# A list scheduler's table of durations: half-width PSUM instructions, tiny scalar ones and the transfer rate

## The chip, the core and the metric

The kernel runs on one core of a Trainium2 chip. The metric is the device time of one execution in microseconds; the time of a kernel is the median of its runs. TensorE (PE) multiplies matrices, and PEld is its weight load, which overlaps it. VectorE (DVE) and ScalarE (ACT) work element by element, GpSimd (POOL) does a few tiny powers, and SyncE (SP) issues every transfer from HBM.

## What is computed

A sequence of 256 tokens of width 1024 goes through two blocks of two layers each, all in fp32.

```python
def first_block(x, ...):             # DEPTH = 2
    for l in range(DEPTH):
        h = hybrid_layer(h, ...)     # norm, w_in, three attentions A, B, C, silu gates, w_out, residual
    return rms_norm(h, final_g)

def second_block(x, ...):
    for l in range(DEPTH):
        h = rms_norm_2(x, mix_pre_norm[l])
        m = hybrid_mixer(h, ...)     # gated delta rule, pooling, retention, three gated branches, w_out
        x = x + rms_norm_2(m, mix_post_norm[l])
        h = rms_norm_2(x, ffn_pre_norm[l])
        x = x + rms_norm_2(swiglu(h, ...), ffn_post_norm[l])
```

## The kernel before

The tokens are two tiles of 128. A weight matrix comes in pieces of two 128-row blocks by up to 512 columns (512 KB), by `piece`: a transfer into a `raw` tile (4 slots), a cast on ACT into `whi` and the remainder on DVE into `wlo` (7 slots each). Every dense product is three matmuls into an `acc` tile of PSUM (3 slots): high by high, high by low and low by high, so that reduced-precision passes add up to nearly fp32. Attention, transposes and the other small products use `sd` tiles of PSUM (5 slots). The stages follow each other: attention layer 1 (to about 115 us), attention layer 2 (to about 250), mixer, feed-forward, mixer, feed-forward.

The program doesn't run in the order in which it is written. `Prog.record` notes every instruction with what it reads and writes, and gives it a duration by `Prog.cost`. `Prog.schedule` then plays the whole program through: each engine takes, of the instructions whose inputs are ready in this play, the one that was recorded first. An instruction is put in its engine's list at the moment the play reaches it; `emit` writes the lists out, and on the chip each engine runs its list strictly in that order. So the durations of `cost`, and in `schedule` the rate of transfers, decide which instruction stands ahead of which, and nothing else. A duration that is too short lets work come early in a list; if the chip is slower there, the engine waits in front of it with later work behind it.

In `cost`, `n` is the number of elements of a partition, `ps` tells that an operand lies in PSUM, and `shift` is an addition for operands that begin on different partitions. A tile of fewer than 128 partitions is called half-width here; such instructions stand in the attention (`kT`, `qT`, `lo` in `attn` and `ab_T`), in `c_in` (96 and 64 partitions) and in the delta rule. Tiny scalar instructions are those on tiles of one to eight columns (`ty`, `r`, `m` in the rows: the normalisations, the exponents' bounds in `attn`, the gate chain of the mixer). In all lists of rows, `b`, `s`, `tg`, `ty`, `m` and so on are the classes of tiles in `Net`. Every engine instruction is issued in `emit`, so one line number, L389, stands for all of them.

Three places of the program come up again. In `attn` each head is: a matmul of scores into `sd`; `TENSOR_REDUCE ty<-sd` on DVE (the maximum); for the masked heads a tiny `TENSOR_SCALAR ty<-ty,m`; two exponentials on ACT into `tg`; transposes `sd<-c,tg` on PE; a cast and a remainder `tg<-sd,tg`; and matmuls `sd<-tg,b`. After the heads, `gate_T` multiplies by the gates: transposes `sd<-c,s`. In `mixer`, the chain from `bas` to `gg` is a score of tiny DVE instructions in a row, and PE's `sd<-m,kk` reads its end. The tile `pv` has one slot: the parameters of the next layer come into it by a transfer that starts when the last reader of the old ones, `b<-b,pv`, is done, and a DVE instruction `pv<-pv` scales them.

## Time and profile before

| | us |
|---|---|
| median of three runs | 1184.35 |
| the runs | 1182.6 to 1185.31 |
| the profiled execution | 1182.21 |
| its span, from the first instruction to the last | 1180.4 |

What lies around the span is 1.8 us. The profile's "busy" of PE takes matmuls with modelled ends that overlap the next one, so a nearly full PE can still lose time between starts. A matmul's real pace is read from the starts of two neighbours: 512 columns take 0.23 us, 384 take 0.17, 256 take 0.12, and a transpose of 128 takes 0.11. The number in brackets behind a row is the idle time ahead of it and what ended it.

### The profile page before, as it was taken

To read this page: it belongs to the slowest core of one execution; us is meant where nothing else is said; L and a number is where in the kernel's file an instruction comes from. 1 tells how busy PE (TensorE), PEld (TensorE's weight loads), DVE (VectorE), ACT (ScalarE), POOL (GpSimd) and SP (SyncE) were. 2 spreads that over 40 slices of the span, in tenths; PEclk is the share of its full clock that TensorE was granted. 3 is DMA by queue.
4 is the path that set the end of the run, shared out by engine and by line. 5 is a ranking of instruction groups with operands and counts; after the bars stand their busy time and mean duration, and the time that the engine had idled before them with its cause. 6 is when DMAs were issued, how large, how long until landed. Compare 5 with 4: busy or idle time off the path is not lost.

```text
span 1180.4 us, 17325 instructions
## 1 busy us (share of the span) xinstructions
PE 1162.6 (98%) x6308; PEld 985.4 (83%) x6308; DVE 888.1 (75%) x1610; ACT 644.7 (55%) x1194; POOL 51.0 (4%) x73
## 2 busy tenths in 40 slices
PE   8999999999999999999999999999999999999997
PEld 6888898878898888888888888898888888888886
DVE  6999899987789787876665638679888777655642
ACT  6777668764465554565454436455554446544531
POOL 1100010000001000000000001000000101000000
PEclk9999999999999999999999999999999999999999
DMA  7335435645373664446644854544654354654651
GB/s 248 123 113 175 148 113 165 195 132 185 108 233 113 208 192 146 152 141 199 204 163 138 274 194 143 162 144 166 226 183 160 108 178 144 201 190 144 226 184 36
DMA packets 64662, 196.54 MB, mean 167 GB/s; under 512 B 11200, under 2 KB 12608, under 8 KB 64576
## 3 DMA queue, kind: packets, MB, share of 16 engines
q1 hardware_dynamic: 64576, 195.44, 51.1%
q8 instruction: 49, 0.80, 0.3%
q14 instruction: 37, 0.30, 0.1%
HBM read 194.10 MB, written 1.05 MB: 165 GB/s over the span
## 4 chain that ended last, share of the span: by engine, by line
PE 82%; DVE 12%; DMA 2%; ACT 2%; issue 2%; POOL 0%; POOLq 0%; DVEq 0%; ACTq 0%
PE acc L389 68%; PE sd L389 15%; DVE wlo L389 4%; DVE b L389 3%; DVE s L389 2%; DVE ty L389 2%; DVE tg L389 1%; DMA raw<-in_wt 1%; ACT whi L389 1%; DMA pv<-in_pv 1%; ACT b L389 0%; DVE m L389 0%; ACT xh L389 0%; ACT s L389 0%; POOL ty L389 0%
## 5 line engine op out<-in xcount | busy, mean ns | idle before, releaser
L389 DVE TENSOR_TENSOR wlo<-raw,whi 128x1024 fp32r<-128x1024 f32 (+4 forms) x380 | 428.0, 1137 | 123.9 <-ACT whi L389 120.9
L389 ACT CAST whi<-raw 128x1024 fp32r<-128x1024 f32 (+4 forms) x380 | 370.6, 984 | 219.2 <-PE acc L389 156.9
L389 PE MATMUL acc<-whi,xh 128*128 128x512 f32 (+4 forms) x1184 | 444.4, 377 | 3.4 <-ACT whi L389 2.6
L389 PE MATMUL acc<-wlo,xh 128*128 128x512 f32 (+4 forms) x1184 | 442.4, 374 | 1.1 <-DVE wlo L389 1.1
L389 PE MATMUL acc<-whi,xl 128*128 128x512 f32 (+4 forms) x1184 | 442.5, 374 | 0.0
L389 PEld LDWEIGHTS acc<-whi,xh 128*128 128x128 f32 x1184 | 223.0, 189 | 40.7 <-ACT whi L389 3.6
L389 PEld LDWEIGHTS acc<-wlo,xh 128*128 128x128 f32 x1184 | 223.3, 189 | 37.9 <-DVE wlo L389 1.9
L389 PEld LDWEIGHTS acc<-whi,xl 128*128 128x128 f32 x1184 | 223.2, 188 | 37.0 <-DVE xl L389 0.7
L389 PE MATMUL acc<-whi,b 128*128 128x512 f32 x328 | 107.0, 396 | 0.0
L389 PEld LDWEIGHTS acc<-whi,b 128*128 128x128 f32 x328 | 61.1, 188 | 14.3 <-ACT b L389 0.4
L389 POOL TENSOR_TENSOR ty<-ty,m 128x4 f32<-128x4 f32 (+3 forms) x34 | 34.9, 1028 | 856.3 <-DVE ty L389 856.3
L389 PE MATMUL sd<-b,b 128*128 128x128 f32 (+3 forms) x464 | 70.1, 289 | 0.1
L389 PE MATMUL acc<-wlo,b 128*128 128x512 f32 x164 | 65.0, 396 | 0.0
L389 PEld LDWEIGHTS sd<-b,b 128*128 128x128 f32 (+2 forms) x464 | 60.4, 190 | 5.4 <-DVE b L389 2.1
L389 ACT ACTIVATE b<-sd 128x512 fp32r<-128x512 f32 (+3 forms) x44 | 23.7, 538 | 63.0 <-PE sd L389 61.8
L389 ACT ACTIVATE s<-acc,r 128x512 f32<-128x512 f32 (+3 forms) x52 | 31.1, 598 | 42.6 <-PE acc L389 40.9
L389 PE MATMUL acc<-xh,whi 128*128 128x256 f32 x192 | 54.0, 281 | 0.0
L389 PE MATMUL acc<-xl,whi 128*128 128x256 f32 x192 | 53.9, 281 | 0.0
L389 PE MATMUL acc<-xh,wlo 128*128 128x256 f32 x192 | 53.8, 280 | 0.0
L389 PE MATMUL sd<-c,s 128*128 128x128 f32 (+2 forms) x260 | 39.9, 273 | 2.8 <-DVE b L389 1.6
L389 DVE SCALAR_TENSOR_TENSOR b<-sd,b 128x512 fp32r<-128x512 f32 (+3 forms) x44 | 26.9, 616 | 17.7 <-ACT b L389 16.7
L389 PEld LDWEIGHTS sd<-c,s 128*128 128x128 f32 (+2 forms) x260 | 30.9, 138 | 10.4 <-DVE s L389 2.6
(178 smaller groups left out, 1278.4 us busy)
## 6 DMA issues: line engine op xcount, KB each, us to landing
raw<-in_wt SPq DMA_DIRECT2D x308, 512.0 KB
raw<-in_wt SPq DMA_DIRECT2D x40, 256.0 KB
raw<-in_wt SPq DMA_DIRECT2D x16, 384.0 KB
raw<-in_wt SPq DMA_DIRECT2D x8, 352.0 KB
b<-in_gains SPq DMA_DIRECT2D x5, 512.0 KB
raw<-in_wt SPq DMA_DIRECT2D x8, 264.0 KB
b<-in_kd SPq DMA_DIRECT2D x2, 512.0 KB
kk<-in_k SPq DMA_DIRECT2D x1, 832.0 KB
```

Of the source, the lines that this page charges most:

```text
L389: o.inst = getattr(eng[o.eng], o.name)(*[real(a) for a in o.args], **{k: real(v) for k, v in o.kw.items()})
```

## The change

Three numbers of the table change. An instruction with a PSUM operand whose result has fewer than 128 partitions gets 110 ns on top, in place of 85 ns or nothing. A `tensor_scalar` on DVE with at most eight columns has a fixed part of 119 ns in place of 69. A transfer moves 280 bytes per ns in place of 350, so that a piece of 512 KB takes 1.87 us of the play's transfer line in place of 1.50. No instruction is added or removed, and no tile changes.

```diff
         shift = 85 if ps and len({a.box[0][0] for a in o.ins + o.outs if a.shape[0] > 1}) > 1 else 0
+        if ps and o.outs[0].shape[0] < P:
+            shift = 110
...
-            return (0.52 if fast else 1.04) * n + 69 + (0 if o.name == "tensor_tensor" else ptr) + shift
+            return (0.52 if fast else 1.04) * n + (119 if n <= 8 and o.name == "tensor_scalar" else 69) + (0 if o.name == "tensor_tensor" else ptr) + shift
...
-                dma = max(dma, hw + 840) + a.free() * a.shape[0] * 4 / 350.0
+                dma = max(dma, hw + 840) + a.free() * a.shape[0] * 4 / 280.0
```

The lists that come of it differ most in the two attention layers (from the first microseconds to about 290 us) and in the mixers; in the feed-forward layers they are the same but for a few pairs. Four places are shown; numbers in tile names differ between the two kernels for the same tile, and the line L389 is L391 afterwards.

Place one, DVE, the end of the last attention of layer 2. `ty_677` before and `ty_672` after hold the maxima of the heads, and `wlo` are remainders of weight pieces. Before:

```order
L389 TENSOR_SCALAR ty_677_2881<-ty_677_2881,m_394_1670 128x2 x2
L389 SCALAR_TENSOR_TENSOR b_700_2971<-s_720_3054,acc_680_2894 128x384
L389 TENSOR_TENSOR s_724_3071<-b_660_2793,m_656_2773 128x384
L389 TENSOR_TENSOR wlo_726_3076<-raw_689_2928,whi_711_3019 128x1024
L389 TENSOR_TENSOR wlo_730_3090<-raw_697_2956,whi_717_3036 128x1024
L389 TENSOR_TENSOR wlo_734_3106<-raw_709_3008,whi_723_3067 128x1024
L389 TENSOR_TENSOR tg_739_3124<-sd_728_3084,tg_733_3101 128x512
L389 TENSOR_TENSOR tg_742_3131<-sd_732_3098,tg_738_3121 128x512
L389 TENSOR_REDUCE ty_677_2881<-sd_736_3110 128x2
L389 TENSOR_TENSOR wlo_745_3145<-raw_713_3024,whi_735_3108 128x1024
L389 TENSOR_TENSOR b_712_3021<-sd_714_3026,s_743_3137 64x256 x2
L389 TENSOR_SCALAR ty_677_2881<-ty_677_2881,m_394_1670 128x2
```

After:

```order
L391 TENSOR_TENSOR wlo_712_3025<-raw_687_2911,whi_706_2996 128x1024
L391 TENSOR_REDUCE ty_672_2859<-sd_709_3009 128x2
L391 TENSOR_TENSOR s_717_3047<-b_658_2805,m_644_2728 128x384
L391 TENSOR_TENSOR tg_719_3054<-sd_713_3029,tg_716_3044 128x512
L391 TENSOR_SCALAR ty_672_2859<-ty_672_2859,m_396_1685 128x2
L391 TENSOR_TENSOR wlo_721_3063<-raw_691_2935,whi_714_3033 128x1024
L391 TENSOR_TENSOR xl_725_3081<-s_670_2853,xh_720_3061 128x2x128
L391 TENSOR_TENSOR xl_725_3081<-s_671_2856,xh_720_3061 128x2x128
L391 TENSOR_TENSOR b_705_2994<-sd_704_2990,s_723_3072 64x256 x2
L391 TENSOR_REDUCE ty_672_2859<-sd_722_3068 128x2
L391 SCALAR_TENSOR_TENSOR b_710_3016<-s_730_3097,acc_663_2829 128x384
L391 TENSOR_SCALAR ty_672_2859<-ty_672_2859,m_396_1685 128x2
```

Both lists end with the tiny instruction on the last head's maxima. Ahead of it, from the first head of this attention on, the list before has seven remainders of 1024 columns, and the one after has three; four have moved behind it.

The same place on PE: `sd_744`, `sd_749` before (`sd_732`, `sd_740` after) are the gates' transposes, `sd_754` (`sd_739`) the last head's. Before:

```order
L389 MATMUL acc_722_3059<-wlo_703_2985,xh_718_3048 128x512
L389 MATMUL acc_722_3059<-whi_686_2918,xl_721_3056 128x512
L389 MATMUL sd_741_3129<-tg_738_3121,b_520_2186 128x256
L389 MATMUL sd_714_3026<-tg_739_3124,b_520_2186 128x256
L389 MATMUL sd_714_3026<-tg_733_3101,b_520_2186 128x256
L389 MATMUL sd_714_3026<-tg_739_3124,b_520_2186 128x256
L389 MATMUL sd_741_3129<-tg_742_3131,b_520_2186 128x256
L389 MATMUL sd_741_3129<-tg_738_3121,b_520_2186 128x256
L389 MATMUL sd_741_3129<-tg_742_3131,b_520_2186 128x256
L389 MATMUL sd_744_3143<-c_6_73,s_688_2926 128x128 x3
L389 MATMUL sd_749_3158<-c_6_73,s_724_3071 128x128 x3
L389 MATMUL sd_754_3171<-c_6_73,tg_750_3161 128x128 x4
```

After:

```order
L391 MATMUL sd_739_3131<-c_6_73,tg_736_3122 128x128 x2
L391 MATMUL sd_740_3134<-c_6_73,s_717_3047 128x128 x2
L391 MATMUL sd_738_3127<-tg_737_3125,b_522_2193 128x256
L391 MATMUL sd_738_3127<-tg_733_3114,b_522_2193 128x256
L391 MATMUL sd_738_3127<-tg_737_3125,b_522_2193 128x256
L391 MATMUL sd_739_3131<-c_6_73,tg_736_3122 128x128 x2
L391 MATMUL sd_740_3134<-c_6_73,s_717_3047 128x128
L391 MATMUL acc_735_3120<-whi_699_2962,xh_720_3061 128x512
L391 MATMUL acc_735_3120<-wlo_701_2980,xh_720_3061 128x512
L391 MATMUL acc_735_3120<-whi_699_2962,xl_725_3081 128x512
L391 MATMUL acc_728_3087<-wlo_712_3025,xh_720_3061 128x512
L391 MATMUL acc_728_3087<-whi_706_2996,xl_725_3081 128x512
```

Before, the transposes of both gates and of the last head, ten in all, stand in one run with the `acc` products ahead of them. After, the transposes come in pieces with other heads' products between them, and the five `acc` products that close the piece stood, for the same pieces of weights, ahead of this place before.

Place two, DVE, the first heads of the same attention. `ty_677` and `ty_672` are the maxima again; the remainders of 768 columns are the four pieces of one chunk of weights. Before (the chunk's first remainder, `wlo_646`, stands 16 rows ahead of the first row shown):

```order
L389 TENSOR_TENSOR wlo_666_2836<-raw_604_2570,whi_620_2628 128x768
L389 SCALAR_TENSOR_TENSOR b_661_2797<-sd_649_2743,b_661_2797 64x3x128
L389 SCALAR_TENSOR_TENSOR b_660_2793<-s_669_2843,acc_657_2775 128x384
L389 TENSOR_TENSOR s_674_2867<-b_563_2411,sd_667_2838 128x256
L389 TENSOR_TENSOR b_655_2767<-sd_649_2743,b_655_2767 64x128 x2
L389 TENSOR_TENSOR s_675_2876<-b_563_2411,sd_670_2845 128x256
L389 TENSOR_REDUCE ty_677_2881<-sd_671_2848 128x2
L389 TENSOR_TENSOR wlo_679_2891<-raw_617_2619,whi_634_2684 128x768
L389 TENSOR_SCALAR ty_677_2881<-ty_677_2881,m_394_1670 128x2
L389 TENSOR_REDUCE ty_677_2881<-sd_676_2879 128x2
L389 TENSOR_TENSOR wlo_684_2911<-raw_637_2695,whi_662_2807 128x768
L389 TENSOR_SCALAR ty_677_2881<-ty_677_2881,m_394_1670 128x2
```

After (the first of the four is `wlo_677`):

```order
L391 TENSOR_REDUCE ty_672_2859<-sd_660_2822 128x2
L391 TENSOR_TENSOR b_646_2741<-sd_654_2773,b_646_2741 64x128 x2
L391 TENSOR_SCALAR ty_672_2859<-ty_672_2859,m_396_1685 128x2
L391 TENSOR_REDUCE ty_672_2859<-sd_673_2861 128x2
L391 TENSOR_TENSOR wlo_677_2878<-raw_609_2587,whi_625_2656 128x768
L391 TENSOR_SCALAR ty_672_2859<-ty_672_2859,m_396_1685 128x2
L391 TENSOR_TENSOR wlo_681_2891<-raw_624_2652,whi_643_2724 128x768
L391 TENSOR_TENSOR tg_685_2906<-sd_678_2880,tg_682_2895 128x512
L391 TENSOR_REDUCE ty_672_2859<-sd_679_2883 128x2
L391 TENSOR_TENSOR wlo_689_2923<-raw_631_2675,whi_650_2759 128x768
L391 TENSOR_SCALAR ty_672_2859<-ty_672_2859,m_396_1685 128x2
L391 TENSOR_TENSOR wlo_692_2937<-raw_656_2785,whi_669_2850 128x768
```

The chunk's first remainder has moved from well ahead of the first head's maxima to behind the second head's, and the other three follow it.

Place three, DVE, the gate chain of the first mixer; `ty_988` before and `ty_987` after carry the polynomial, and `b_952<-b_952,pv` is the last reader of the old `pv`. Before (the row that follows is `pv<-pv`):

```order
L389 TENSOR_TENSOR ty_985_4217<-ty_977_4183 128x8
L389 TENSOR_TENSOR wlo_986_4220<-raw_964_4124,whi_983_4202 128x1024
L389 TENSOR_SCALAR ty_988_4233<-ty_985_4217 128x8
L389 TENSOR_TENSOR b_952_4065<-b_952_4065,pv_753_3169 128x512
L389 SCALAR_TENSOR_TENSOR ty_988_4233<-ty_988_4233,ty_985_4217 128x8
L389 TENSOR_TENSOR wlo_990_4246<-raw_972_4155,whi_987_4224 128x1024
L389 SCALAR_TENSOR_TENSOR ty_988_4233<-ty_988_4233,ty_985_4217 128x8 x4
L389 TENSOR_TENSOR wlo_994_4273<-raw_978_4186,whi_992_4255 128x1024
L389 SCALAR_TENSOR_TENSOR ty_988_4233<-ty_988_4233,ty_985_4217 128x8 x2
L389 TENSOR_TENSOR wlo_997_4293<-raw_984_4213,whi_995_4278 128x1024
L389 SCALAR_TENSOR_TENSOR ty_988_4233<-ty_988_4233,ty_977_4183 128x8
L389 SCALAR_TENSOR_TENSOR ty_988_4233<-ty_965_4129,ty_988_4233 128x8
```

After (`pv<-pv` stands one row further on):

```order
L391 TENSOR_TENSOR b_952_4065<-b_952_4065,pv_743_3143 128x512
L391 TENSOR_TENSOR ty_979_4190<-ty_979_4190,ty_969_4147 128x8
L391 TENSOR_TENSOR wlo_982_4210<-raw_960_4104,whi_978_4188 128x1024
L391 TENSOR_TENSOR ty_985_4226<-ty_979_4190 128x8
L391 TENSOR_SCALAR ty_987_4231<-ty_985_4226 128x8
L391 TENSOR_TENSOR wlo_988_4234<-raw_964_4125,whi_984_4216 128x1024
L391 SCALAR_TENSOR_TENSOR ty_987_4231<-ty_987_4231,ty_985_4226 128x8 x4
L391 TENSOR_TENSOR wlo_991_4260<-raw_971_4153,whi_989_4242 128x1024
L391 SCALAR_TENSOR_TENSOR ty_987_4231<-ty_987_4231,ty_985_4226 128x8 x3
L391 SCALAR_TENSOR_TENSOR ty_987_4231<-ty_987_4231,ty_979_4190 128x8
L391 TENSOR_TENSOR wlo_994_4285<-raw_981_4196,whi_992_4268 128x1024
```

From the first row of the chain on, the last reader of `pv` has moved ahead of the reciprocal's successor, with fewer remainders ahead of it, and one remainder that stood ahead of `pv<-pv` now stands behind it.

## Rows read from the trace of the kernel before

**Rows 1.** The page's first part: busy time, share of the span, instructions.
```profile
PE 1162.6 (98%) x6308; PEld 985.4 (83%) x6308; DVE 888.1 (75%) x1610; ACT 644.7 (55%) x1194; POOL 51.0 (4%) x73
```
**Rows 2.** Stretches: length; busy PE, PEld, DVE, ACT, POOL; PE clock; DMA share; GB/s.
```profile
40.00:120.00 80.00, 78.66 (x509) 68.84 (x508) 77.95 (x160) 64.09 (x160) 1.93 (x2) 1.00 0.41 131
160.00:233.00 73.00, 72.33 (x484) 64.76 (x483) 71.73 (x145) 59.15 (x148) 1.93 (x2) 1.00 0.52 168
...
240.00:300.00 60.00, 60.00 (x286) 48.71 (x285) 48.01 (x85) 34.51 (x63) 2.22 (x4) 1.00 0.49 155
...
520.00:700.00 180.00, 180.00 (x861) 149.40 (x860) 110.07 (x136) 89.64 (x123) 2.57 (x3) 1.00 0.60 195
```
**Rows 3.** Instructions by shape: count, busy us, mean ns, idle before.
```profile
L389 DVE TENSOR_TENSOR wlo<-raw,whi 128x1024 fp32r<-128x1024 f32 x308 | 373.3, 1222 | 116.2 <-ACT whi L389 113.6
L389 DVE TENSOR_TENSOR wlo<-raw,whi 128x768 fp32r<-128x768 f32 x16 | 15.2, 952 | 0.1
...
L389 DVE TENSOR_SCALAR ty<-ty 128x1 f32<-128x1 f32 x22 | 4.6, 211 | 18.1 <-ACT s L389 18.1
...
L389 DVE SCALAR_TENSOR_TENSOR ty<-ty,ty 128x8 f32<-128x8 f32 x18 | 3.0, 164 | 0.3
...
L389 ACT CAST b<-sd 64x128 fp32r<-64x128 f32 x32 | 8.4, 262 | 4.6 <-DVE b L389 4.3
```
**Rows 4.** DVE, in order of time around 229 to 236 us: start, length, instruction.
```profile
228.67 3.49 DVE L389 TENSOR_TENSOR wlo<-raw,whi 128x1024 fp32r<-128x1024 f32 x3
...
233.87 1.22 DVE L389 TENSOR_TENSOR wlo<-raw,whi 128x1024 fp32r<-128x1024 f32 x1
...
235.89 0.23 DVE L389 TENSOR_SCALAR ty<-ty,m 128x2 f32<-128x2 f32 x1
```
**Rows 5.** PE at the same place, then the stretch after it (columns as in rows 2).
```profile
236.01 0.52 PE L389 MATMUL sd<-c,s 128*128 128x128 f32 x3 [1.64 <-DVE b L389]
236.84 1.15 PE L389 MATMUL sd<-c,tg 128*128 128x128 f32 x4 [0.31 <-ACT tg L389]
...
236.60:240.00 3.40, 3.16 (x10) 2.40 (x11) 3.38 (x11) 1.73 (x7) 0.00 (x0) 0.50 0.60 214
```
**Rows 6.** DVE and PE, in order of time, 172 to 213 us.
```profile
172.85 0.60 PE L389 MATMUL sd<-c,tg 128*128 128x128 f32 x4
...
202.43 0.95 DVE L389 TENSOR_TENSOR wlo<-raw,whi 128x768 fp32r<-128x768 f32 x1
...
203.70 0.44 PE L389 MATMUL sd<-c,tg 128*128 128x128 f32 x2 [0.25 <-ACT tg L389]
...
211.26 0.41 PE L389 MATMUL sd<-c,s 128*128 128x128 f32 x2 [0.40 <-DVE s L389]
...
212.41 0.34 PE L389 MATMUL acc<-wlo,xh 128*128 128x384 f32 x1
```
**Rows 7.** PE in attention layer 1, its waits at three places.
```profile
58.88 0.44 PE L389 MATMUL sd<-c,tg 128*128 128x128 f32 x2 [0.15 <-ACT tg L389]
...
87.12 0.66 PE L389 MATMUL sd<-c,s 128*128 128x128 f32 x4 [0.38 <-DVE s L389]
...
106.18 0.50 PE L389 MATMUL acc<-whi,xh 128*128 128x512 f32 x1 [0.32 <-ACT xh L389]
```
**Rows 8.** DVE and PE at the gate chain of the first mixer, and two later waits.
```profile
348.92 0.49 DVE L389 TENSOR_SCALAR pv<-pv 128x640 f32<-128x640 f32 x1 [1.14 <-DMA pv<-in_pv]
...
348.77 0.28 PE L389 MATMUL acc<-xh,whi 128*128 128x256 f32 x1
349.75 1.06 PE L389 MATMUL sd<-m,kk 128*128 128x8 f32 x8 [0.70 <-DVE m L389]
...
364.43 0.71 PE L389 MATMUL sd<-b 128*128 128x128 f32 x4 [0.55 <-DVE b L389]
...
822.53 0.71 PE L389 MATMUL sd<-b 128*128 128x128 f32 x4 [0.28 <-DVE b L389]
```
**Rows 9.** DVE and PE at two places of the mixer where nothing waits long now.
```profile
272.83 1.23 DVE L389 TENSOR_TENSOR wlo<-raw,whi 128x1024 fp32r<-128x1024 f32 x1 [3.21 <-ACT whi L389]
...
503.20 0.62 PE L389 MATMUL sd<-c,b 128*128 128x128 f32 x4
```
**Rows 10.** PE near the start, attention layer 1.
```profile
21.38 0.50 PE L389 MATMUL acc<-wlo,xh 128*128 128x512 f32 x1 [0.60 <-DVE wlo L389]
...
22.50 0.44 PE L389 MATMUL sd<-c,s 128*128 128x128 f32 x2 [0.39 <-DVE s L389]
```

## The prediction, made before the changed kernel was run

> **What bounds the kernel now.** I read the engines' busy times first. PE is busy for 98% of the span, DVE for 75%, ACT for 55% [rows 1]. A reordering takes no work from PE; all it can give back is time in which PE waits or runs at the lower clock. So the second view is the table of stretches [rows 2]: PE's busy time fills the stretch in the feed-forward (180.00 of 180 us) and between 240 and 300 us, and there is nothing to gain there. In the attention it shares the bound with DVE, which is busy 77.95 of 80 us and 71.73 of 73: there the order on DVE decides when PE gets its input. Third come the waits of PE in order of time. At the places that the change moves they are few: 1.64 and 0.31 us at 236 and 237 us [rows 5], 0.25 and 0.40 in layer 2 [rows 6], 0.15, 0.38 and 0.32 in layer 1 [rows 7], 0.70, 0.55 and 0.28 in the mixers [rows 8], 0.60 and 0.39 near the start [rows 10]. That makes 5.97 us. With them goes one stretch at the lower clock that the change can reach: from 236.60 to 240.00 us the granted clock is 0.50, 1.2 GHz, behind the wait of 1.64 us [rows 5]. Everything the change can win is about 7.5 us of 1182, and what the brackets leave out.
>
> **Are the new durations nearer to the chip?** Yes, in part. A tiny scalar instruction takes 211 ns [rows 3]; the fixed part of 119 ns in place of 69 goes towards that and stays short of it. A half-width copy from PSUM on ACT takes 262 ns [rows 3], and 110 more on top of the old price comes close. The remainders of 1222 and 952 ns [rows 3] are not touched. So in the play, the chains of the attention's heads grow longer and the weights come later; what matters is which remainders then stand ahead of which head.
>
> **The change, part by part.** I followed the moved instructions of both lists with the durations and start times of the trace before, from one wait to the next. Gains are positive.
>
> A, the end of attention in layer 2 (place one): the second gate's transposes wait 1.64 us for DVE, then the last head's wait 0.31 us [rows 5]. On DVE the tiny instruction on the last head's maxima runs at 235.89, behind seven remainders of 1024 columns, three of them in one run at 228.67 and one more at 233.87 [rows 4]. Four of the seven now stand behind it: 4 x 1.222 = 4.9 us, so DVE is there by far more than 1.95 us earlier, and PE, which has handed five matmuls to a later place, arrives only some 1.8 us earlier (five of 0.23 from start to start, and the waits of layer 2 below). Both waits go: 1.95. With the long wait gone I expect the clock to stay up: from 236.60 to 240.00 PE was busy 3.16 us at 0.50, work of 1.58 us at the full clock; the other 1.58 come back. A = +3.5. Its bounds: 0, if the four remainders are merely late afterwards, to 3.5.
>
> B, the first heads of the same attention (place two): the waits of 0.25 and 0.40 [rows 6] have fewer remainders ahead of them now and go, +0.65. Against that, the chunk's first remainder moves behind the second head's maxima. In the new list 29 instructions stand ahead of it that stood behind; by their durations in the trace they make 12.0 us. The remainder ran at 202.43 and took 0.95; the matmul that reads the chunk starts at 212.41 [rows 6], a slack of 9.0 us. Work that leaves the front of all of them gives 1.7 back: 9.0 + 1.7 - 12.0 = -1.3, a new wait of about 1.25. The transposes at 172.85 [rows 6] come a little ahead of their exponentials: -0.5. B = 0.65 - 1.75 = -1.1. Bounds: -1.75 (no old wait goes) and +0.65 (no new one comes).
>
> C, layer 1: the three waits [rows 7], 0.85 together, each have between one and six remainders fewer ahead of their releaser; one new wait of about 0.3 near 95 us appears, a remainder of 1.22 us being put ahead of a gate there whose slack is 0.9. C = +0.6; bounds 0 and 0.85.
>
> D, the mixers (place three): DVE stands 1.14 us before `pv<-pv` for the transfer [rows 8], with the end of the gate chain behind it, and PE's `sd<-m,kk` waits 0.70 us at 349.75. In the new list the last reader of the old `pv` stands earlier by two tiny instructions and a remainder, so the transfer starts earlier, and one remainder of 1.222 us leaves the front of `pv<-pv`. PE gets there 0.6 us earlier by what it gained in this layer, which costs part of it: relief 0.65, between 0 and the row's whole. The wait of 0.55 at 364.43 loses 0.43, and the one of 0.28 at 822.53 all of it, each with a remainder less ahead. D = 0.65 + 0.43 + 0.28 = +1.4; bounds 0 and 1.5.
>
> On tiny instructions one rule can be weighed here. The scalar_tensor_tensor steps of that chain, 128x8, take 164 ns, hardly less than the 211 of a tensor_scalar on one column [rows 3]; the change lifts only the second. The Trainium skill says in "VectorE: DVE Perf Modes", section "The TRN2 errata — SBUF-src ops pay a fixed extra latency per instruction", that such an operation pays a fixed cost whatever its size. By that the chain would still be planned too short, D would lack its 0.65, and the sum below would be 3.35.
>
> E, places where nothing waits long now: at 272.83 a remainder waits 3.21 us for its cast [rows 9] and PE reads it some 0.8 us behind its end; PE is some 1.6 us earlier by A and B, which would cost 0.83. The cast is itself released by PE for the most part and comes earlier with it, so I take half: -0.4 (0 to -0.83). The transposes at 503.20 [rows 9] and their twins in the second mixer come one half-width addition too early, a third of a microsecond each: -0.7. E = -1.1; bounds 0 and -1.6.
>
> F, the start: 0.60 and 0.39 [rows 10] become one wait of about 1.1, for one remainder that is put ahead of the others: -0.1; bounds +1.0 (both go) and -1.2 (a whole further remainder of 1.22 stands ahead).
>
> G: a bracket leaves out that the pipeline of matmuls drains. At 349.75 the start is 0.98 us behind the start of the matmul at 348.77, whose own pace is 0.12: 0.86 lost, 0.70 in the bracket [rows 8], 0.16 more. Some nine waits go and four come: 5 x 0.16 = +0.8, between 0 and 1.4.
>
> Nothing is charged for SP's issues: the weights come later in the play, but the chip's transfers start when slots come free, and the DMA share is 0.41 to 0.60 in all these stretches [rows 2]. If that cover were gone, a late piece would cost PE up to the 1.87 us the play now gives it.
>
> Sum: 3.5 - 1.1 + 0.6 + 1.4 - 1.1 - 0.1 + 0.8 = +4.0. The profiled execution took 1182.21 us, 2.14 below the median; the changed one would take 1178.2, its span 1176.4, and the median 1184.35 - 4.0 = 1180.35, say **1180.4**.
>
> **The rivals.** First: the DVE work is only moved (same). Where DVE is busy 71.73 of 73 us [rows 2], four remainders that leave the front of one wait are behind it for the next; PE reads those weights a few microseconds later. The clock stretch and the waits of A then come back at another place. For it: DVE has only 1.3 us of idle time there. Against it: from 240 us on DVE is busy 48.01 of 60 us, so that the four remainders find room. Without A the sum is 4.0 - 3.5 = 0.5: 1183.85.
>
> Second: the new waits lower the clock (same). The one wait of 1.64 us here was followed by 3.4 us at 0.50 [rows 5], which cost 1.58. If the new waits of about 1.25 us, near 21 us and near 212 us, do the same, 3.2 go again: 4.0 - 3.2 = 0.8, 1183.5. Against it: 0.60 and 0.39 us so near each other [rows 10] brought no stretch of that kind. The Trainium skill, in "TensorE: Matmul & The Clock Gate", section "Part 1: The HAM clock gate (the "warmup" mystery)", says that the clock has just these two states and follows how busy the engine has been of late; the trace agrees with the two states, and it leaves open which of the waits is enough.
>
> Third: place two is dearer than I think (slower). The four remainders of 768 columns of the chunk now stand one behind another behind the heads' maxima. If the heads' maxima themselves come late (they wait for PE, and PE waits for the remainders), each of the four comes 0.95 plus about 0.7 of other DVE work late, 1.64, and PE pays each: 6.6 us, and 1.6 for a clock that then falls, in place of the 1.25 counted: 4.0 - 6.9 = -2.9, 1187.3. For it: DVE has no idle time there to catch up. Against it: the chunk is read once, so a wait for its first remainder covers part of the others. It turns the sign as soon as PE's waits between 205 and 220 us make more than 1.25 + 4.0 = 5.3 us, the clock's loss included, and shows as slower from 2.4 more on.
>
> **How the numbers follow.** A measurement of this kernel can tell about 0.2%, 2.4 us, from no change: faster is below 1182.0, slower above 1186.7. The forecast has 0.56: A moves 4.9 us of work against 1.95 of waits, but B and E hang on slacks of a microsecond. The first rival has 0.14, the second 0.08, the third 0.22. So faster 0.56, same 0.22, slower 0.22. If all the terms were at their good ends, 8.9 us would go, at their bad ends 4.6 would come; half of the way from 4.0 to 8.9 is 6.5, 1177.9, and the spread of the runs before, 1.75 below the median, is taken off: low 1176.1. Above, the third rival's 1187.3 has to be taken in, and 0.3 for the runs: high 1187.6.
>
> **What would show it.** In the changed trace: A, no wait above 0.5 us at PE's gate transposes near 234 us and a clock of 1.00 up to 300 us; B, one wait of about 1.25 for DVE `wlo` near 211 us and none at the two old places; C, waits at 87 and 106 us below 0.1; D, `sd<-m,kk` waiting under 0.1 near 347 us, and DVE before `pv<-pv` hardly at all; E, a wait of about 0.4 near 271; F, one of about 1.1 near 21; no difference of PE's losses in the two feed-forward layers. I would be wrong on the sign if several waits for `wlo` follow each other between 205 and 245 us, and on the whole approach if the feed-forward, whose lists hardly differ, changed its length by more than 0.5 us.

## The result and the profile after

The changed kernel takes 1190.48 us (1189.19 to 1191.40, 4 runs) beside 1184.34 us of the kernel before on the same chip: 1.0063 times as long by all runs of both, 95% interval 1.0050 to 1.0075 (the two medians alone give 1.0052). The forecast was 1180.4 us, faster, with a range of 1176.1 to 1187.6. It is slower, and outside the range. The profiled execution has a span of 1187.4 us, 7.0 more than before, with the same instructions. Engine totals (answers to [rows 1]):

```profile
PE 1165.3 (98%) x6308; PEld 988.4 (83%) x6308; DVE 889.3 (75%) x1610; ACT 644.2 (54%) x1194; POOL 50.8 (4%) x73
```

The same stretches as [rows 2] (length; busy PE, PEld, DVE, ACT, POOL; PE clock; DMA share; GB/s). In the attention PE lost where it had been nearly full, 76.42 of 80 us and 69.61 of 73, and DVE is less busy than before, not more:

```profile
40.00:120.00 80.00, 76.42 (x497) 67.69 (x497) 77.21 (x160) 62.98 (x159) 1.93 (x2) 1.00 0.42 130
160.00:233.00 73.00, 69.61 (x465) 63.46 (x465) 67.18 (x139) 54.14 (x140) 2.26 (x2) 0.98 0.48 147
520.00:700.00 180.00, 180.00 (x860) 149.07 (x859) 109.36 (x137) 88.72 (x123) 3.12 (x4) 1.00 0.58 191
```

Where the time went is read by laying the two traces side by side: at a point where PE has done exactly the same set of instructions in both, the difference of the two times is what the list has cost so far. In the table, the time that each kernel takes over before in four parts of the program (times of before; one profile each; minus is faster).

| kernel | to 300 us (attention) | 347 to 367 and 804 to 820 (gate chains) | 448 to 516 (end of mixer 1) | 860 to 972 (end of mixer 2) | all |
|---|---|---|---|---|---|
| changed | +2.0 | -1.7 | +3.6 | +2.1 | +7.3 |
| E1 mixers only | +0.8 | -1.6 | +3.5 | +1.9 | +4.5 |
| E2 attention only | +4.1 | +1.1 | +0.1 | +0.2 | +6.1 |
| E3 rate only | -1.0 | -1.7 | +3.4 | +3.5 | +5.2 |
| E4 old rate | +2.4 | +0.1 | +0.1 | 0.0 | +3.0 |
| E5 changed, links off the line | +4.0 | -1.7 | +2.0 | +1.5 | +7.6 |
| E6 rate only, links off the line | -0.3 | -1.7 | +0.4 | +1.0 | +0.1 |
| E7 before, slow links | -0.7 | +0.8 | +16.9 | +9.9 | +26.6 |
| E8 tiny only | -3.3 | +0.9 | +0.3 | +0.3 | -1.7 |
| E9 before, light remainders | -6.8 | +0.9 | 0.0 | 0.0 | -6.2 |
| E10 changed, light remainders | +1.8 | -1.7 | +3.6 | +2.0 | +7.3 |
| E11 half-width only | +1.6 | +0.4 | +0.6 | +0.6 | +3.4 |
| E12 tiny only, links off the line | -3.9 | -0.9 | +2.1 | +0.9 | -1.9 |

Differences of one or two microseconds in the first column can't be put down to a list. E1 and E7 have the attention's list of before and stand at +0.8 and -0.7; E2 and E5 have that of the changed kernel and stand at +4.1 and +4.0, where it has +2.0. In the gate chains E9 loses 0.9 with the list of before. At the ends of the mixers, E9 with the list of before and E10 with the changed one repeat within 0.1.

So the changed kernel lost at two kinds of place: the attention's heads, and the ends of the mixers. In the attention, PE in order of time (start, length, instruction, idle before and its releaser), and the stretch behind the last two, with its clock:

```profile
94.88 0.44 PE L391 MATMUL sd<-c,s 128*128 128x128 f32 x2 [1.05 <-DVE s L391]
96.23 0.51 PE L391 MATMUL sd<-b,b 128*128 128x256 f32 x2 [0.92 <-DVE b L391]
...
97.48 0.44 PE L391 MATMUL sd<-c,tg 128*128 128x128 f32 x2 [0.31 <-ACT tg L391]
...
215.90 0.50 PE L391 MATMUL sd<-b,b 128*128 128x256 f32 x2 [1.38 <-DVE s L391]
...
218.06 0.44 PE L391 MATMUL sd<-c,tg 128*128 128x128 f32 x2 [1.22 <-DVE ty L391]
...
218.00:222.00 4.00, 3.93 (x16) 3.51 (x17) 3.70 (x7) 1.96 (x7) 0.00 (x0) 0.57 0.52 140
```

At the end of the first mixer, PE of the kernel before, then of the changed one, at the same instructions. Before, 29 products lie between the transposes `sd<-c,b` of 483.35 and the first product that reads their copy, at 490.48; afterwards none lies between 491.60 and 493.02, and PE waits for the cast on ACT. This is the first place. At the second, `tg` is read out of the `acc` tile that PE's next product at 501.18 needs; 23 instructions (19 products and 4 transposes) lie there before, from 497.68 on, and 5 (one product and 4 transposes) afterwards, from 498.48 on:

```profile
483.35 0.62 PE L389 MATMUL sd<-c,b 128*128 128x128 f32 x4
...
490.48 0.39 PE L389 MATMUL acc<-whi,b 128*128 128x512 f32 x1
```

```profile
491.60 0.60 PE L391 MATMUL sd<-c,b 128*128 128x128 f32 x4
493.02 0.50 PE L391 MATMUL acc<-whi,b 128*128 128x512 f32 x1 [0.82 <-ACT b L391]
...
498.48 0.60 PE L391 MATMUL sd<-c,b 128*128 128x128 f32 x4
499.64 0.66 PE L391 MATMUL sd<-c,b 128*128 128x128 f32 x4 [0.32 <-DVE b L391]
501.18 0.47 PE L391 MATMUL acc<-whi,xh 128*128 128x512 f32 x1 [0.88 <-DVE tg L391]
```

What comes late there is the delta rule's chain. Ahead of it stand links: small transfers from one `b` tile to another, each waiting for the one before, that SP issues between the weights of later products. They are two groups of eight in each mixer. SP's queue at the last links of the first mixer, changed, then before, with the DVE instruction that reads the last one:

```profile
444.05 0.33 SPq L391 DMA_DIRECT2D raw<-in_wt  x1
444.43 0.64 SPq L391 DMA_DIRECT2D b<-b  x1
445.77 3.65 SPq L391 DMA_DIRECT2D raw<-in_wt  x2
449.47 0.63 SPq L391 DMA_DIRECT2D b<-b  x1
450.83 0.33 SPq L391 DMA_DIRECT2D raw<-in_wt  x1
451.21 0.63 SPq L391 DMA_DIRECT2D b<-b  x1
...
457.30 1.29 DVE L391 TENSOR_TENSOR b<-b,kk 128x512 f32<-128x512 f32 x2
```

```profile
443.64 0.64 SPq L389 DMA_DIRECT2D b<-b  x1
445.06 0.33 SPq L389 DMA_DIRECT2D raw<-in_wt  x1
445.44 0.63 SPq L389 DMA_DIRECT2D b<-b  x1
...
450.59 1.29 DVE L389 TENSOR_TENSOR b<-b,kk 128x512 f32<-128x512 f32 x2
```

From the first link to this reader the kernel before takes 72.05 us (378.55 to 450.59) and the changed one 77.52 (379.77 to 457.30).

### The profile page after: what moved, and what is told of

Its sections match the earlier page's. It is cut to its first block, busy times and chain, and to the rows that moved or that the text cites. A ratio compares the mean times of both kernels' runs of the same rounds, so it can differ in the third digit from the quotient of the medians.

```text
span 1187.4 us, 17305 instructions
## 1 busy us (share of the span) xinstructions
PE 1165.3 (98%) x6308; PEld 988.4 (83%) x6308; DVE 889.3 (75%) x1610; ACT 644.2 (54%) x1194; POOL 50.8 (4%) x73
## 4 chain that ended last, share of the span: by engine, by line
PE 91%; DVE 6%; ACT 2%; issue 1%; DMA 0%; POOLq 0%; DVEq 0%; ACTq 0%
PE acc L391 73%; PE sd L391 18%; DVE s L391 2%; DVE wlo L391 1%; DVE b L391 1%; DVE ty L391 1%; ACT xh L391 0%; DMA raw<-in_wt 0%; ACT s L391 0%; ACT whi L391 0%; ACT b L391 0%; DVE tg L391 0%; DVE xl L391 0%; ACT tg L391 0%; DVE x L391 0%
## 5 line engine op out<-in xcount | busy, mean ns | idle before, releaser
L391 DVE TENSOR_TENSOR wlo<-raw,whi 128x1024 fp32r<-128x1024 f32 (+4 forms) x380 | 427.4, 1135 | 122.5 <-ACT whi L391 119.6
L391 ACT CAST whi<-raw 128x1024 fp32r<-128x1024 f32 (+4 forms) x380 | 369.4, 982 | 206.0 <-PE acc L391 145.3
L391 PE MATMUL acc<-whi,xh 128*128 128x512 f32 (+4 forms) x1184 | 444.4, 378 | 3.6 <-ACT whi L391 1.7
L391 PE MATMUL acc<-wlo,xh 128*128 128x512 f32 (+4 forms) x1184 | 442.9, 375 | 0.8 <-DVE wlo L391 0.8
L391 PE MATMUL acc<-whi,xl 128*128 128x512 f32 (+4 forms) x1184 | 442.2, 375 | 0.0
L391 PEld LDWEIGHTS acc<-whi,xh 128*128 128x128 f32 x1184 | 223.2, 189 | 41.6 <-ACT whi L391 2.3
L391 PEld LDWEIGHTS acc<-wlo,xh 128*128 128x128 f32 x1184 | 223.6, 189 | 37.6 <-DVE wlo L391 1.6
L391 PEld LDWEIGHTS acc<-whi,xl 128*128 128x128 f32 x1184 | 223.5, 189 | 36.3 <-issue 0.2
L391 PE MATMUL acc<-whi,b 128*128 128x512 f32 x328 | 107.5, 396 | 0.8 <-ACT b L391 0.8
L391 PEld LDWEIGHTS acc<-whi,b 128*128 128x128 f32 x328 | 61.5, 188 | 15.0 <-ACT b L391 1.1
L391 PE MATMUL sd<-b,b 128*128 128x128 f32 (+3 forms) x464 | 70.6, 290 | 2.5 <-DVE s L391 1.4
L391 POOL TENSOR_TENSOR ty<-ty,m 128x4 f32<-128x4 f32 (+3 forms) x34 | 33.0, 975 | 862.4 <-DVE ty L391 862.4
L391 PEld LDWEIGHTS sd<-b,b 128*128 128x128 f32 (+2 forms) x464 | 61.2, 192 | 7.7 <-DVE b L391 2.9
L391 PE MATMUL acc<-wlo,b 128*128 128x512 f32 x164 | 64.9, 396 | 0.0
L391 ACT ACTIVATE b<-sd 128x512 fp32r<-128x512 f32 (+3 forms) x44 | 23.6, 537 | 63.2 <-PE sd L391 62.5
L391 ACT ACTIVATE s<-acc,r 128x512 f32<-128x512 f32 (+3 forms) x52 | 31.1, 597 | 45.1 <-PE acc L391 43.7
L391 PE MATMUL acc<-xh,whi 128*128 128x256 f32 x192 | 54.1, 282 | 0.0
L391 PE MATMUL acc<-xh,wlo 128*128 128x256 f32 x192 | 54.1, 282 | 0.0
L391 PE MATMUL acc<-xl,whi 128*128 128x256 f32 x192 | 53.9, 281 | 0.0
L391 PE MATMUL sd<-c,s 128*128 128x128 f32 (+2 forms) x260 | 41.1, 274 | 3.5 <-DVE s L391 2.6
L391 PEld LDWEIGHTS sd<-c,s 128*128 128x128 f32 (+2 forms) x260 | 31.1, 138 | 11.4 <-DVE s L391 4.0
L391 DVE SCALAR_TENSOR_TENSOR b<-sd,b 128x512 fp32r<-128x512 f32 (+3 forms) x44 | 27.0, 616 | 18.2 <-ACT b L391 17.5
```

What stands on the lines that cost most here:

```text
L391: o.inst = getattr(eng[o.eng], o.name)(*[real(a) for a in o.args], **{k: real(v) for k, v in o.kw.items()})
```

## The experiments

E1 to E4 split the change, by place and by number. `new` is true for instructions of the part that has the new numbers; the first mixer begins just ahead of instruction 2600.

```diff
+        new = len(self.ops) >= 2600      # E1; E2: < 2600
-        if ps and o.outs[0].shape[0] < P:
+        if new and ps and o.outs[0].shape[0] < P:
...
+        o.rate = 280.0 if len(self.ops) >= 2600 else 350.0
```

**E1, mixers only.** 

> The three new numbers of the table hold only for instructions recorded from the first mixer on; both attention layers keep the old ones, and with them the old lists to about 260 us. Theory COVER: a play with slower transfers runs out of ready weight products in the mixers and puts the products that read a fresh copy right behind the transposes that feed it; the chip then waits there. The changed kernel lost 5.2 us more than the kernel before from 350 us on, whatever came ahead, so this one takes about 1189.5 us (1188.5 to 1190.5), with the waits near 490 to 502 and 958 us in its trace. Rival SHIFT: the mixers' lists are fair and only meet a DVE and buffers that the attention left in another state; then this kernel stays within 1.2 us of before, at most 1185.5, and the waits near 490 us are absent.

Measured: 1185.87 us beside 1182.35, ratio 1.0023 (1.0011 to 1.0036). The expectation, 1188.5 to 1190.5, was missed: it is 3.5 us over before in place of 5.2. The ends of the mixers lose 3.5 and 1.9 us, all waits near 490 to 502 and 958 us are there, with the attention of before ahead of them. The loss is the mixers' own.

**E2, attention only.** 

> The reverse: the new numbers hold for the instructions recorded up to the end of the attention, the mixers and feed-forward layers keep the old ones and the old lists. Theory COVER: what the attention lost and won in the changed kernel is all that is left, +2.0 us at 290 us, so about 1186.3 us (1185.3 to 1187.3). Rival SHIFT: the loss of the mixers comes along, at least 1189.

Measured: 1187.97 beside 1182.35, ratio 1.0039 (1.0026 to 1.0052). The mixers' ends lose 0.1 and 0.2; rival SHIFT falls. But the time, 1185.3 to 1187.3 expected, was missed: the attention costs 4.1 us with the very lists that cost 2.0 in the changed kernel's profile; the last section has part of the reason.

E3 has the rate of 280 alone, E4 the two durations with the rate of 350.

**E3, rate only.** 

> Only the transfer rate of the play is 280 bytes per ns; the half-width and tiny durations are the old ones. The lists put 1.2 and 0.9 us of products between the transposes and the product that reads their copy at the two places near 490 to 502 us, where before has 6.7 and 4.8, and 0.9 at the twin of the second in the second mixer. Theory COVER: 2 to 4 us are lost in the mixers, and the attention, whose list is new once more, adds between -1 and +3: 1188 us (1185.5 to 1191). Rival DURATIONS: the half-width and tiny numbers did it, and this kernel is within 1.5 us of before in the mixers, with about 1185.

Measured: 1187.07 beside 1182.35, ratio 1.0038 (1.0026 to 1.0051), 3.4 and 3.5 us lost at the ends, 6.9 together where 2 to 4 were expected.

**E4, old rate.** 

> The half-width and the tiny durations of the changed kernel, with transfers at 350 bytes per ns as before. The lists keep 4.9, 3.5 and 3.5 us of products at the three places of the mixers where the changed kernel has 0.0, 0.7 and 1.1. Theory COVER: the mixers lose at most 0.7 us against before, or gain up to 1 by the waits near 350 and 364 us; the attention, whose list is new once more, gives between -2 and +2: 1184 us (1182 to 1186.5). Rival DURATIONS: the mixers lose 3 us or more as in the changed kernel, 1187 to 1190.

Measured: 1184.87 beside 1182.35, ratio 1.0021 (1.0012 to 1.0030), 0.1 and 0.0 at the ends. The mixers' loss comes from the rate; the attention, 2.4 us slower, loses without it too, as far as one profile tells.

E5 to E7 ask by which way the rate does it. Which transfers are late in the play can be chosen: in E5 and E6 the links no longer queue on the weights' line, in E7 the links alone are made slower in the kernel before.

```diff
+                if o.ins and o.outs and o.outs[0].vt.cls == o.ins[0].vt.cls == "b":
+                    o.end = hw + 840 + 1500        # E5, E6, E12
+                else: (the two lines that stood here)
...
+                    o.end += 1000                  # E7, behind those two lines
```

**E5, the changed table with the links off the line.** 

> The changed table, but in the play the sixteen small transfers of a mixer from one b tile to another (the links of the delta rule's gather, each waiting for the one before) don't queue on the weights' transfer line; the weights still move at 280 bytes per ns. The attention's lists are those of the changed kernel word for word. Theory LINKS (the slower line made the links late in the play, so that the products of weights were put ahead of the chain and none was left at the mixers' ends): the list has 6.9 us of products at the first place near 490 us where the changed kernel has none, 6.4 at the twin of the second in the second mixer, and still 0.7 at the second place near 500. The mixers' ends (448 to 516 and 860 to 972 us of before) lose at most 1.2 us where the changed kernel loses 5.7, and the kernel is 1 to 3.5 us over before. Rival WEIGHTS (weights at 280 alone empty the list): the ends still lose 4 us or more, and the kernel is 5 to 7 us over before.

Measured: 1189.28 beside 1182.34, ratio 1.0051 (1.0038 to 1.0063). The ends lose 3.5 us together in place of 5.7: neither forecast. The first place has 30 products again and no wait; the second, near 502 us, still has 5 instructions and loses 0.6. New waits near 455 and 912 us take 0.5 each, and one near 412, outside the ends, 0.7.

**E6, the rate alone with the links off the line.** 

> The transfer rate of 280 with the old durations, as in the run with the rate alone, and the links off the line. Cover at the three places: 9.0, 6.4 and 4.8 us of products. Theory LINKS: the ends of the mixers lose at most 0.5 us, where the run with the rate alone lost 6.8; the attention keeps that run's list and its -1.0, the gate chains near 350 and 806 us give about -1.5: 2 to 3 us below before. Rival WEIGHTS: 2 us or more above before.

Measured: 1181.78 beside 1182.34, ratio 0.9983 (0.9970 to 0.9995). The ends lose 1.4 us together where E3 loses 6.8; at most 0.5 had been expected, and the kernel is 0.6 us below before in place of 2 to 3. With the weights at 280 just the same, four fifths of the rate's loss are gone.

**E7, slow links in the kernel before.** 

> The kernel before, with one cost doubled the other way: its own table, transfers at 350, but each of the sixteen small links takes 1 us more in the play. The lists differ from before in the mixers alone. Cover at the three places: 0.0, 3.7 and 0.9 us, against 6.7, 4.8 and 4.8. Theory LINKS: the ends of the mixers lose 3 us or more in the first mixer and 2 or more in the second, 5 to 9 us over before. Rival WEIGHTS: weights at 350 keep the lists full, within 1 us of before.

Measured: 1204.73 beside 1182.34, ratio 1.0188 (1.0168 to 1.0208), 16.9 and 9.9 us lost at the ends, more than twice what was expected, with the attention's lists untouched. Part of that is the clock: in the profiled execution it was 0.83 from 460 to 505 us. PE shows a wait of 0.7 to 1.7 us at nearly every step of the chain:

```profile
479.77 6.42 PE L391 MATMUL sd<-b,b 128*128 128x128 f32 x40 [1.69 <-DVE b L391]
...
502.35 1.09 PE L391 MATMUL sd<-c,b 128*128 128x128 f32 x4 [1.47 <-DVE b L391]
504.11 0.79 PE L391 MATMUL acc<-whi,b 128*128 128x512 f32 x1 [0.68 <-ACT b L391]
```

WEIGHTS falls, LINKS stands: a number that makes the chain late in the play empties the list behind it.

**E8, tiny only.** 

> Only the fixed part of tiny tensor_scalar instructions is 119. The mixers' covers are 5.3, 4.4 and 4.4 us, so by theory LINKS their ends lose at most 0.4. It is one more list for the attention: theory SCATTER (in stretches where DVE is full every change of the table gives another place where PE waits, the truer number included) gives anything between -1 and +4 us at 300 us; rival TRUER (the truer a duration, the fewer waits): below 0 at 300 us. In all -2 to +4 us against before.

Measured: 1179.76 beside 1182.34, ratio 0.9973 (0.9963 to 0.9984). This version beats both kernels, and all of its gain lies in the attention, 3.3 us at 300 us: more than SCATTER allowed for. The sign is that of TRUER, but most of the durations changed here moved away from the chip (see below, the aim of the table), so TRUER isn't borne out; E11 speaks against it too.

E9 and E10 ask what the attention's waits are made of. The lists stay; the remainders of both attention layers become cheaper.

```diff
+            if o.eng == "DVE" and o.outs[0].vt.cls == "wlo" and o.pri < 2600:
+                o.inst = nc.vector.tensor_scalar(real(o.args[0]), real(o.args[2]), 0.0, None, op0=ALU.mult)
+                continue
```

**E9, before with light remainders.** 

> The lists of the kernel before, but in both attention layers each remainder is a product of the cast piece with zero, which leaves the remainders' share out of the attention's dense products (its output differs by that). Such an instruction takes about half the time on DVE; the lists and the play don't change. Theory FULL (in the attention DVE is full, and where its list is late PE waits): the waits of PE for DVE there, 0.3 to 1.8 us each, go, and 300 us of before are reached 3 to 7 us earlier. Rival CHAIN (PE waits for the length of a head's or gate's chain, which the order puts too near): at most 1.5 us earlier.

Measured: 1176.62 beside 1181.94, ratio 0.9960 (0.9945 to 0.9975); 6.8 us faster at 300 us, within FULL's 3 to 7. But the waits mostly stay: those of 0.25, 0.40, 0.38, 0.31 and 0.32 are 0.23, 0.39, 0.29, 0.31 and 0.32, and only the one of 1.64 falls, to 1.10. Of the 6.8 us, 1.8 are gained in the first 25 us, and some 0.9 come because the clock is 1.00 behind 231 us in this run; the rest comes in small steps. FULL's sum came, its cause only in part.

**E10, changed with light remainders.** 

> The same with the lists of the changed kernel. Theory FULL: the waits near 46, 95 and 216 us go with the clock's fall behind them, the changed kernel gains 5 to 10 us by 300 us, and the difference to the lists of before with light remainders is under 1.2 us there, where it is 2 to 4 with full ones; the mixers' loss of some 5 us stays. Rival CHAIN: the difference at 300 us stays at 2 us or more.

Measured: 1189.04 beside 1181.94, ratio 1.0062 (1.0047 to 1.0077); at 300 us as late as the changed kernel, +1.8. DVE is busy for 68.28 us of 40 to 120 in place of 77.21, and these five waits of PE are what they were, to 0.01 us:

```profile
93.49 0.44 PE L394 MATMUL sd<-c,s 128*128 128x128 f32 x2 [1.05 <-DVE s L394]
94.84 0.50 PE L394 MATMUL sd<-b,b 128*128 128x256 f32 x2 [0.91 <-DVE b L394]
...
96.09 0.50 PE L394 MATMUL sd<-c,tg 128*128 128x128 f32 x2 [0.32 <-ACT tg L394]
...
215.84 0.51 PE L394 MATMUL sd<-b,b 128*128 128x256 f32 x2 [1.38 <-DVE s L394]
217.99 0.44 PE L394 MATMUL sd<-c,tg 128*128 128x128 f32 x2 [1.21 <-ACT tg L394]
...
40.00:120.00 80.00, 76.72 (x494) 68.20 (x493) 68.28 (x157) 62.17 (x158) 1.93 (x2) 0.98 0.36 111
```

So it is not the remainders that stand in front of these waits, and FULL falls for them. CHAIN's number came, but its cause is not shown. DVE is busy for 6.12 of the 6.50 us from 89.0 to 95.5 in the changed kernel, and for just as much of the same stretch in E10, on the heads', rotations' and gates' own instructions. The `s<-b,m` for which PE waits at 94.88 had its last input at 70.85 and a free tile at 86.5; it stood in DVE's list behind other instructions:

```profile
93.17 0.60 DVE L391 TENSOR_TENSOR b<-sd,b 64x128 fp32r<-64x128 f32 x2
93.80 0.56 DVE L391 SCALAR_TENSOR_TENSOR b<-sd,b 64x384 fp32r<-64x384 f32 x1
94.39 0.43 DVE L391 TENSOR_TENSOR s<-b,m 128x256 f32<-128x256 f32 x1
```

How much of these waits is DVE's order of its small instructions, and how much the length of a chain from PE over DVE and ACT back to PE, E10 doesn't separate.

**E11, half-width only.** 

> Only the half-width PSUM instructions cost 110 more. The lists of the mixers have 6.9 us of products at the first place near 490 us and its twin, but 0.7 us at the second place near 500 us and its twin. Theory LINKS and cover: no wait at the first place, 0.6 to 1.1 us at the second in both mixers. Theory SCATTER for the attention: another value between -1 and +4 us at 300 us. In all 0 to 5 us over before.

Measured: 1186.48 beside 1181.94, ratio 1.0047 (1.0031 to 1.0064). The waits of the attention near 95 and 216 us of the changed kernel have counterparts here, at the same instructions, with this number alone; at the mixers' ends the first places don't wait, and the second, with five instructions of cover, lose 0.6 us each:

```profile
89.66 0.44 PE L391 MATMUL sd<-c,s 128*128 128x128 f32 x2 [1.83 <-DVE s L391]
90.89 0.75 PE L391 MATMUL sd<-b,b 128*128 128x256 f32 x2 [0.79 <-DVE b L391]
...
212.59 0.50 PE L391 MATMUL sd<-b,b 128*128 128x256 f32 x2 [2.06 <-DVE b L391]
214.50 0.69 PE L391 MATMUL acc<-wlo,xh 128*128 128x384 f32 x1 [0.98 <-DVE wlo L391]
...
498.86 0.47 PE L391 MATMUL acc<-whi,xh 128*128 128x512 f32 x1 [0.43 <-DVE tg L391]
```

**E12, tiny only with the links off the line.** 

> The tiny durations alone, the fastest so far at -2.6 us, with the links of the mixers off the weights' line. Covers of 9.0, 6.4 and 6.4 us in place of 5.3, 4.4 and 4.4. Theory LINKS: the run with the tiny durations loses only 0.2 us at the ends of the mixers, so there is nothing left to win: within 0.7 us of it, 2 to 3.3 us below before. Rival: chains that run ahead cost DVE's or SP's order elsewhere, 1 us or more above the tiny run.

Measured: 1180.16 beside 1181.94, ratio 0.9987 (0.9977 to 0.9996). It doesn't beat E8: the chain now runs early, and 2.1 us go in the first mixer, 1.2 of them at 445 us, where PE waits 1.01 us for a `b` of the chain itself. Expected were 2 to 3.3 us below before; it is 1.8, where E8 is 2.6 below its own. That is too much for LINKS, which allowed 0.7 between the two, and too little for the rival, which asked for 1; the rival's cost is still seen in the 2.1.

## Why the prediction was wrong, step by step

**The aim of the table.** The prediction said that the new durations come nearer to the chip, and that 119 for a tiny instruction stays short of its 211 ns. That was a misreading: 211 is what the trace shows from start to end, and the table needs what an instruction keeps the engine from the next. DVE starts the next while the one before still shows: in the changed kernel 0.12 us after a tiny one of 0.22, in the kernel before 0.07 us after one of 0.17:

```profile
96.55 0.22 DVE L391 TENSOR_SCALAR ty<-ty,m 128x2 f32<-128x2 f32 x1
96.67 0.95 DVE L391 TENSOR_TENSOR wlo<-raw,whi 128x768 fp32r<-128x768 f32 x1
```

```profile
336.81 0.17 DVE L389 TENSOR_SCALAR ty<-ty 128x8 f32<-128x8 f32 x1
336.88 0.17 DVE L389 TENSOR_SCALAR m<-m 128x8 f32<-128x8 f32 x1
```

By these distances the new number is the right one for 22 of the 118 tiny `tensor_scalar`s, those with the 211 ns: they are 121 to 131 ns apart and are priced 120 in place of 70. Sixty others are 60 to 73 ns apart where nothing waits, which was their old price; the new one is 120 to 123. The remaining 36, `ty<-ty,m` among them, carry 61 ns on top in the table for a column of another tile; they are 126 to 138 apart, were priced at 131 to 138 and are now at 181 to 188. So for most of them the table moved away from the chip.

The half-width number comes nearer in most cases: two casts on ACT take 0.53 together, and their starts lie 0.27 apart, beside a new price of 268 ns. It doesn't for the ones on DVE with 96 partitions (some 600 ns apart, 601 before, 711 now).

```profile
94.40 0.53 ACT L391 CAST b<-sd 64x128 fp32r<-64x128 f32 x2 [0.87 <-DVE b L391]
```

The rate doesn't either: from 9 to 15 us, with the DMA engines full, the kernel before moved 353 GB/s, which is the old 350 and not 280:

```profile
9.00:15.00 6.00, 5.50 (x25) 5.20 (x26) 5.01 (x13) 5.26 (x15) 1.27 (x1) 0.72 1.05 353
```

Nearer or not did not decide the sign: the tiny number, mostly farther from the chip, makes the kernel 0.27% faster by itself (E8), and the half-width one, mostly nearer, 0.47% slower (E11).

**A** was right in mechanism and in size: the last gates and the last head don't wait, and the stretch runs at the full clock (answers to [rows 5]). From 235.5 to 240.2 us PE lost 3.9 us between starts before and less than 0.1 afterwards, forecast 3.5.

```profile
236.00:241.00 5.00, 5.00 (x32) 4.28 (x31) 4.92 (x13) 5.00 (x14) 0.00 (x0) 1.00 0.41 152
```

**B** is the first step that failed. The two old waits went (1.07 us by starts). The forecast put one wait of 1.25 near 212 us, for `wlo` and the product that reads it. What came were 1.38 and 1.22 at 216 and 218 us for `s` and for the head's exponentials, and the clock at 0.57 behind them: some 4.5 us, and 0.6 and 0.5 at 175 and 181. For `wlo` PE waited nowhere from 200 to 235 us: the chunk's first remainder ended at 218.93 and was read at 220.29. I had counted the slack of the instruction that moved most; the ones that mattered were the heads' own. The `s` of 215.90 ran on DVE 0.91 us after its inputs were there, and the maximum ahead of 218.06 ran 1.46 us after its own.

**C** failed likewise: forecast +0.6, measured -1.4. The place near 95 us was named with 0.3; it has three waits in a row, 2.9 us by starts. Two more, 0.50 and 0.44 near 46 us, were not named. As in B, a remainder was priced; what came late near 95 us were small instructions of DVE's list (E10).

**D** was right: DVE doesn't wait ahead of `pv<-pv`, and PE no longer in front of `sd<-m,kk`; 1.7 us in both mixers, forecast 1.4. But the sum is right partly by luck: the wait of 0.55 at 364.43 only fell to 0.46, the one of 0.28 at 822.53 is 0.34 now, and the gain came from the two gate chains (answers to [rows 8]).

```profile
349.01 0.49 DVE L391 TENSOR_SCALAR pv<-pv 128x640 f32<-128x640 f32 x1
...
350.25 0.95 PE L391 MATMUL sd<-m,kk 128*128 128x8 f32 x8
366.06 0.71 PE L391 MATMUL sd<-b 128*128 128x128 f32 x4 [0.46 <-DVE b L391]
```

**E** is the larger failure: -1.1 forecast, -5.7 measured. The part near 272 us didn't come: from 265 to 280 us PE loses nothing. The other part had the neighbourhood and not the price: "a third of a microsecond each". The transposes named, those of 503.20 before, wait for nothing now, at 502.43; the waits stand up to ten microseconds ahead of them, at 493.02, 499.64 and 501.18, and in the second mixer at 960.67, each worth 0.6 to 1.1 us by starts. I had moved every instruction by what its own predecessors gained or lost, one at a time. Where the list leaves no product between a step and the next, every step of the chain is paid in full. And I took the transfer rate for a matter of weights alone, "Nothing is charged for SP's issues"; it also sets when the links are thought to land (E6, E7).

**F**: -0.1 forecast, -0.7 measured; the two waits became one of 1.54, in place of 1.1 (answer to [rows 10]). The -0.7 is that of the whole first 25 us; the waits alone went from 1.32 to 1.70 by starts.

```profile
21.90 0.70 PE L391 MATMUL sd<-c,s 128*128 128x128 f32 x3 [1.54 <-DVE s L391]
```

Together the measured terms, with B's small items against its two old waits, are 3.9 - 4.5 - 1.4 + 1.7 - 5.7 - 0.7 = -6.7 of the 7.3. They leave out what lies outside the four parts of the table, 1.3 us, and make 2.7 of the attention, where side by side gives 2.0; G has no measured term of its own, since all are taken from start to start. B, C and E all came out beyond the bounds that they were given, -1.75, 0 and -1.6, so that even the sum of all bad ends, 1188.9 us, lies under the measured time.

**The rivals.** The third had the sign and the place, 205 to 220 us, but neither the cause, a wait for `wlo`, nor the sum: 4.5 us there are less than the 5.3 at which it would have decided alone. The first had the effect, that the time of A comes back 20 us earlier in the program, but not the cause: the four remainders are not what stands in front of the new waits (E10). The second was right about the clock at 218 us. No rival spoke of the mixers' ends, where the largest single miss lies. That the feed-forward would not move held: 0.45 us from 516 to 700.

Left open: how much of the mixers' loss is SP's list and how much is PE's. In both mixers the links are longer on the chip. In the first they take 5.5 us more up to the reader. In the second, the instruction that needs the last link is the second of its two readers: it starts 74.4 us after the first link, behind a wait of its own, where before it took 71.8. No run gives the changed kernel's links one list and its products the other.

```profile
915.73 0.69 DVE L391 TENSOR_TENSOR b<-b,kk 128x512 f32<-128x512 f32 x1 [2.73 <-DMA b<-b]
```

At the second mixer's end 9 and 7 instructions are left at the two places where 29 and 23 were; the 9 still cover the wait, the 7 don't.

## What to carry to other kernels

When a list is made by a greedy play, look in the new list for the places where an engine's own chain comes back to it (transposes, copy, product) and count the instructions that lie between. At the first place of a mixer's end none left 0.7 to 0.8 us of wait, and five or more hid it; at the second, where the way back is longer, four to seven cost 0.3 to 1.9 us, and 17 or more nothing. Slacks of single instructions, taken from the old trace, find the waits that go and miss those that come. A truer table need not be a better list, nor a less true one a worse: each number has to be tried alone.

## What the runs showed of the hardware

The same list doesn't meet the same clock each time. Behind the waits near 95 us, identical in the changed kernel and in E2 (94.88 and 95.68, 1.30 us by starts in both), the clock is 1.00 in one and 0.64 in the other:

```profile
97.00:100.00 3.00, 2.69 (x20) 2.43 (x20) 3.00 (x6) 2.20 (x8) 0.00 (x0) 1.00 0.44 128
```

```profile
97.00:100.00 3.00, 2.66 (x13) 2.34 (x14) 3.00 (x6) 1.02 (x4) 0.00 (x0) 0.64 0.17 48
```

Of the 2.1 us between the two in the attention 1.3 are lost from 90 to 118 us, where this is, and 0.9 in the first 25 us. Whole runs differ too: of the eleven runs of E6, four took 1177.5 to 1179.1 us at a mean clock of 0.998 or 0.999, and seven 1181.4 to 1183.6 at 0.995 or 0.996. Which wait the clock followed in the longer runs isn't shown, since one run of E6 was profiled.

A link costs far more than its 8 KB: SP's issues of neighbouring links are 2.5 to 2.9 us apart where nothing else stands between but a weight or two (425.19, 427.70, 430.59 and 433.44 before). At the 353 GB/s of 9 to 15 us the bytes alone would take 0.02 us, by my estimate.
